# Five edits to the attention stage of a hybrid retention and dilated-attention decoder step

## The chip, the core and the metric

The kernel runs on one core of one Trainium2 chip. The metric is the device time of one execution in microseconds (us), the median of the runs. The engines go by the names that the profile gives them: PE is TensorE (matmuls; PEld its weight loads), DVE is VectorE, ACT is ScalarE, POOL is GpSimd, and SP is SyncE, which issues most DMAs.

## What is computed

One step of a one-layer decoder, for a prompt of 512 tokens and a sample group of 8 sequences with 8 new tokens each, 576 tokens in all. An RMSNorm and one input projection (1024 to 3584 columns) feed two groups of heads. Eight heads do retention (chunks of 128, a state that is carried on). Eight heads of width 64 do softmax attention over a mixture of dilated windows, with a distance penalty:

```python
BRANCHES = ((128, 1), (512, 4), (2048, 16))
for window, dil in BRANCHES:
    dist = dil * jnp.arange(window // dil + 1, dtype=jnp.int32)
    local = q_pos[:, None] - dist[None, :] - k_start
    ...
    s = jnp.einsum('bqhd,bqnhd->bhqn', qf, kg) - slopes[:, None, None] * dist
```

The prompt attends to its own keys; the sample attends to 1024 cached keys and values of each sequence and to its new ones. Both groups are concatenated, projected back and added; a gated feed-forward layer with a causal convolution of width 3 follows (1024 to 2 x 2816 and back), and a last RMSNorm. Outputs are the tokens, the retention states, the key and value caches with the new rows at their end, and the convolution's state. All data is fp32.

## The kernel before

Activations stand with features on partitions and the 576 tokens along the free dimension. A dense product (L254) splits weights and activations into a high and a low part of type fp32r and adds three products, high x high, high x low and low x high; each weight block of 128 x 128 meets two halves of 288 tokens, so a step of one 128-row block is six matmuls. ACT makes the high part of a weight chunk (L219), DVE the low part (L229), SP loads it (L211).

Work is written out as streams (Python generators) that a small planner, `Merge`, interleaves when the program is built. Each `yield a, b` says how much TensorE time was just written and how long to wait for other engines; a third number, where there is one, is the progress that counts in place of the first. Streams with an amount of work left (`mg.add(in_proj(), 130.0e3)`, `attn_prompt` 32.7e3, `attn_sample` 59.6e3) are served so that their progress relative to what is left stays equal. A stream that yields `None` waits until something else has moved on. Every engine then executes its instructions strictly in the order that the planner wrote.

After the retention part, three such streams share TensorE from about 150 to 336 us of the span:

- `in_proj` goes on with the projection. For the third and fourth pair of heads its attention sections wait until all six attention units of the pair two before (four of the prompt, two of the sample) are written.
- `attn_prompt` runs `attn_unit(hp, i)` for each pair of heads and each block i of 128 queries, sixteen units, at most two at once. A unit with i > 0 splits its queries into a high part `qa` and a rest `ql`, multiplies them with split keys (L764 with 128 rows, L766 with 64 rows each for the two heads), takes the softmax (exponential on ACT L780, reciprocals on DVE L783, both heads' weights scaled on POOL L785), transposes the weights (L791) and multiplies with the values (L804). n = 128 (i + 1) is the number of keys.
- `attn_sample` runs eight units of four sequences. For each sequence it loads a key tile `kc` (three buffers) and a value tile `vc` (six buffers) of 384 KB from the cache, each with three DMAs issued by SP (L861, L863), and transposes the keys (L877, copies L878). Then the unit multiplies queries with keys (L887), takes the softmax, transposes the weights (L910, and L911 for the 64 columns of new keys) and multiplies with the values (L923: four matmuls side by side in column groups of 32; the last step has only the 64 rows of new values). Just before a unit, POOL copies the new keys of its four sequences into their key tiles (L977).

`natural` transposes a section of 576 tokens back to rows (L495: four full blocks and one of 64 columns); `store_window` writes the new cache rows, with one DMA for each of the 8 sequences of the sample (L507). PSUM has two tiles of type `d` and four of type `m`; `room` and `give` count the latter. From 336 us on the program is output projection and feed-forward, and nothing in it is edited.

Of the kernel before, what the change touches and what calls it, by code (L numbers as in the profile page):

```python
# [18 lines left out]
P = 128  # L19
D = 1024  # L20
NP = 512
# [125 lines left out]
def decoder_step(ctx, tc, a):  # L147
# [147 lines left out]
    def rows_of(j):  # L295
        return (P, slice(j * P, (j + 1) * P)) if j < 4 else (NS, slice(NP, T))
# [191 lines left out]

    def natural(src, dst):

        yield from room(2)
        p1, p2 = mtile(), mtile()
        for j in range(5):
            r, s = rows_of(j)
            pe.transpose((p1[:, s] if j < 4 else p2[:NS, :P]), src[:, s], ident)  # L495
        yield 550.0, 300.0
        act.copy(dst[:, 0:4], p1.rearrange("p (j c) -> p j c", j=4))
        dve.tensor_copy(dst[:NS, 4], p2[:NS, :P])
        give(2)

    def store_window(nat, which, hp):
        c = slice(hp * P, (hp + 1) * P)
        op_ = a[f"o_w{which}_p"].rearrange("a (j p) h d -> p (a j) (h d)", p=P)[:, :, c]
        sp.dma_start(op_, nat[:, 0:4])
        os_ = a[f"o_w{which}_s"]
        for b in range(B):
            sp.dma_start(os_[b, PAST:PAST + TS].rearrange("t h d -> t (h d)")[:, c], nat[b * TS:(b + 1) * TS, 4])  # L507

# [12 lines left out]
    def in_post(m, ps):  # L521
# [12 lines left out]
        elif sec < 4:  # L534
# [10 lines left out]
            if sec in (1, 2):  # L545
                n = rp.tile([P, 5, P], F32, name=f"n{sec}", tag=f"n{sec}", bufs=2)
                yield from natural(t, n)
                r["kv"[sec - 1]] = n
# [3 lines left out]
        else:  # L552
# [8 lines left out]
            else:  # L561
                dve.tensor_mul(t, y, rstd_b)
                yield 0.0, 1700.0
                n = atp.tile([P, 5, P], F32, name=f"n{sec}", tag=f"n{sec}", bufs=1 if sec == 5 else 2)
                yield from natural(t, n)
                if sec == 6:
# [166 lines left out]
    half, used = {}, {}  # L733
    pbs, O, flying = {}, {}, {"p": 0, "s": 0}

# [5 lines left out]
    def attn_unit(hp, i):  # L741
# [3 lines left out]
        if i:  # L745

            q_ = A[hp][4][:, i * P:(i + 1) * P]
            qa = [kvb[0].tile([P, P], F32R, name=f"qa{h2}", tag=f"qa{h2}", bufs=2) for h2 in range(2)]
            ql = kvb[0].tile([P, P], F32R, name="ql", tag="ql", bufs=2)
            for h2, q in halves():  # L750
                act.copy(qa[h2][q], q_[q])
                act.copy(qa[h2][other(h2)], q_[q])
            yield 0.0, 1000.0
            for h2, q in halves():
                dve.tensor_sub(ql[q], q_[q], f32(qa[h2][q]))
            yield 0.0, 500.0
# [5 lines left out]
        else:  # L762
            for h2 in range(2):
                pe.matmul(pss[h2][:, :n], qa[h2], kk[hp][h2][:, :n], start=True, stop=False)  # L764
            for h2, q in halves():
                pe.matmul(pss[h2][:, :n], ql[q], kk[hp][h2][q, :n], start=False, stop=True)  # L766
        for ps in pss:
# [14 lines left out]
        for ps, s, c in S:  # L782
            dve.reciprocal(c[:, 2:3], c[:, 1:2])  # L783
        for ps, s, c in S:
            pool.tensor_scalar(s[:, :n], s[:, :n], c[:, 2:3], 1.0, op0=OP.mult, op1=OP.mult)  # L785
        yield 0.0, 2.5 * n + 300.0
        yield from room(2)
# [27 lines left out]

    kk, scored = {}, {}

# [32 lines left out]
    def attn_sample():  # L850
# [3 lines left out]
        def load(u, x, which):  # L854
# [5 lines left out]
            cols = slice(hp * P, (hp + 1) * P)  # L860
            sp.dma_start(t[:, 2:6], c[512:].rearrange("(j p) h d -> p j (h d)", p=P)[:, :, cols])  # L861
            for j in range(2):
                sp.dma_start(t[:, j], c[256 * j:256 * (j + 1)].rearrange("(m u) h d -> m u (h d)", u=16)[:, 0:8, cols])  # L863
            return t
# [5 lines left out]
        def keys(u, x):  # L870
# [8 lines left out]
            del K[u, x]  # L879
            KT[u, x] = kt  # L880

        def unit(u):
# [26 lines left out]
            for j in range(6):  # L909
                pe.transpose(ps[:, j * P:(j + 1) * P], s[:, j * P:(j + 1) * P], ident)  # L910
            pe.transpose(ps[:NS, KEYS:KEYS + P], s[:, SK:], ident)  # L911
            yield 770.0, 200.0
            pt = kvb[0].tile([P, 7, P], F32, name="spt", tag="spt", bufs=1)
            dve.tensor_copy(pt[:, :3].rearrange("p j q -> p (j q)"), ps[:, :384])
            act.copy(pt[:, 3:6].rearrange("p j q -> p (j q)"), ps[:, 384:KEYS])
            act.copy(pt[:NS, 6], ps[:NS, KEYS:KEYS + P])  # L916
            yield 0.0, 2200.0
            yield from room(1)
            ps = mtile()
            for j in range(7):  # L920
                for x in range(4):
                    n, v = (P, V[u, x][:, j]) if j < 6 else (NS, A[hp]["v"][:NS, 4])
                    pe.matmul(ps[x * 32:(x + 1) * 32, :P], pt[:n, j, x * 32:(x + 1) * 32], v, start=j == 0, stop=j == 6,  # L923
                              tile_position=(0, x * 32))
                if j == 3:
                    yield 900.0, 0.0
# [35 lines left out]
        for u in range(8):  # L962
            hp, g = units[u]
            for x in range(4):
                yield from room(2)
                keys(u, x)
                give(2)
                yield 660.0, 1600.0
                ahead(4 * u + x + 4, "k")
# [5 lines left out]
            for x in range(4):  # L975
                b = 4 * g + x
                pool.tensor_copy(KT[u, x][:, KEYS:], A[hp][5][:, NP + b * TS:NP + (b + 1) * TS])  # L977
            flying["s"] += 1
            mg.add(unit(u), None, 600.0)
            yield 0.0, 1000.0, 4100.0  # L980

# [17 lines left out]
    kvx = mid.enter_context(ExitStack())  # L999
    kvb.append(kvx.enter_context(tc.tile_pool(name="kv", bufs=2, reuse_waits="tile")))  # L1000

    MIX = [4, 5, 6, 7, 0, 1, 2, 3]
# [321 lines left out]
```

## Time and profile before

| what | value |
|---|---|
| runs of the kernel before | 829.95, 831.85, 833.71 us; median 831.85 us |
| profiled execution | 832.6 us, its span 830.8 us |
| mean granted TensorE clock | 0.994 |
| PE, share of the span with a matmul in flight | 98% |
| DVE / ACT / POOL busy | 50% / 36% / 18% |
| DMA | 128.68 MB, mean 155 GB/s |

The profiled execution is 0.75 us above the median and 1.8 us longer than its span. Matmuls overlap, so that a busy PE is not a PE at its best: what one costs is read from the distance between starts. PE also stands still while its sequencer waits, and then the weight load (PEld) of the next matmul shows the wait.

### The profile page before, as it was taken

How to read it: one execution, taken by the hardware profiler on the slowest of the kernel's cores; microseconds unless marked ns; L12 is line 12 of the kernel's file. 1: busy time of each engine (PE TensorE's matmuls, PEld its weight loads, DVE VectorE, ACT ScalarE, POOL GpSimd, SP SyncE). 2: the span in 40 equal slices, each digit the busy share in tenths (PEclk: the TensorE clock that was granted, in tenths of full speed). 3: DMA queues.
4: the chain of work that ended last, by engine and by line, in shares of the span. 5: the costliest groups of instructions: out<-in, count | busy, mean ns of one | idle time of the engine just before them, and what ended most of it. 6: DMA issues, size and time to landing. Idle time of an engine off the chain costs nothing.

```text
span 830.8 us, 15970 instructions
## 1 busy us (share of the span) xinstructions
PE 813.8 (98%) x6559; PEld 772.2 (93%) x6559; DVE 412.5 (50%) x792; ACT 295.3 (36%) x511; POOL 148.0 (18%) x234
## 2 busy tenths in 40 slices
PE   7999999999999999999999999999999999999995
PEld 6999999887887888999999999999999999999995
DVE  4664555665546456754545455432235545453333
ACT  5422232554446367333223323311223323342222
POOL 1321202011111113023122212100012322210111
PEclk9999999999999999999999999999999999999998
DMA  9354653658787774455265554543334445543213
GB/s 269 102 173 125 203 175 97 185 158 236 217 219 197 219 212 121 110 177 179 78 201 178 178 174 125 168 140 89 93 102 153 152 152 178 171 156 96 71 52 115
DMA packets 180247, 128.68 MB, mean 155 GB/s; under 512 B 15424, under 2 KB 176848, under 8 KB 179661
## 3 DMA queue, kind: packets, MB, share of 16 engines
q1 hardware_dynamic: 179021, 93.75, 40.3%
q10 hardware_dynamic: 928, 33.63, 11.2%
q8 instruction: 52, 0.85, 0.4%
q0 software_dynamic: 224, 0.28, 0.1%
q14 instruction: 22, 0.18, 0.1%
HBM read 121.52 MB, written 39.66 MB: 194 GB/s over the span
## 4 chain that ended last, share of the span: by engine, by line
PE 96%; ACT 1%; DVE 1%; DMA 0%; POOL 0%; issue 0%; ACTq 0%; DVEq 0%; POOLq 0%
PE d L254 75%; PE m L877 2%; PE m L923 2%; PE d L451 2%; PE m L804 1%; PE d L887 1%; PE m L791 1%; PE m L495 1%; PE px L410 1%; PE m L1214 1%; PE px L254 1%; PE m L663 1%; PE m L764 1%; PE d L910 1%; PE m L766 1%; PE m L627 1%
## 5 line engine op out<-in xcount | busy, mean ns | idle before, releaser
L219 ACT ACTIVATE whi<-wraw 128x1024 fp32r<-128x1024 f32 (+2 forms) x114 | 110.6, 970 | 364.9 <-issue 182.6
L229 DVE TENSOR_TENSOR wlo<-wraw,whi 128x1024 fp32r<-128x1024 f32 (+2 forms) x114 | 126.7, 1112 | 120.4 <-ACT whi L219 117.0
L254 PE MATMUL d<-bhi,whi 128*128 128x288 f32 x768 | 173.3, 307 | 0.0
L254 PE MATMUL d<-bhi,wlo 128*128 128x288 f32 x768 | 164.3, 295 | 0.0
L254 PE MATMUL d<-blo,whi 128*128 128x288 f32 x768 | 163.9, 295 | 0.0
L254 PE MATMUL d<-hhi,whi 128*128 128x288 f32 x704 | 150.9, 296 | 0.0
L254 PE MATMUL d<-hhi,wlo 128*128 128x288 f32 x704 | 150.8, 296 | 0.0
L254 PE MATMUL d<-hlo,whi 128*128 128x288 f32 x704 | 150.7, 296 | 0.0
L254 PEld LDWEIGHTS d<-bhi,whi 128*128 128x128 f32 x768 | 121.5, 189 | 5.2 <-issue 3.6
L254 PEld LDWEIGHTS d<-bhi,wlo 128*128 128x128 f32 x768 | 123.3, 188 | 0.0
L254 PEld LDWEIGHTS d<-blo,whi 128*128 128x128 f32 x768 | 123.2, 188 | 0.0
L254 PEld LDWEIGHTS d<-hhi,whi 128*128 128x128 f32 x704 | 113.4, 189 | 0.1
L254 PEld LDWEIGHTS d<-hhi,wlo 128*128 128x128 f32 x704 | 113.4, 189 | 0.0
L254 PEld LDWEIGHTS d<-hlo,whi 128*128 128x128 f32 x704 | 113.4, 189 | 0.0
L1122 DVE TENSOR_TENSOR ue<-d,rstd_b 128x512 f32<-128x512 f32 x22 | 15.2, 691 | 74.6 <-PE d L254 74.6
L1141 POOL TENSOR_TENSOR g<-g,cv 128x512 f32<-128x512 f32 x20 | 25.7, 1287 | 142.1 <-DVE g L1138 136.7
L785 POOL TENSOR_SCALAR s<-s,sc 128x128 f32<-128x128 f32 (+3 forms) x32 | 18.2, 575 | 141.1 <-DVE sc L783 139.9
L1038 POOL TENSOR_TENSOR acc<-acc,sq 128x576 f32<-128x576 f32 x13 | 20.9, 1607 | 104.2 <-ACT sq L1037 104.2
L1127 POOL COPY cout<-ue 128x2 f32<-128x2 f32 x22 | 5.7, 258 | 137.8 <-DVE ue L1122 137.8
L878 DVE COPY kt<-m 128x384 f32<-128x384 f32 x32 | 17.8, 556 | 22.4 <-PE m L877 21.2
L878 ACT COPY kt<-m 128x384 f32<-128x384 f32 x32 | 15.3, 477 | 38.4 <-PE m L877 36.8
L877 PE MATMUL m<-ident,kc 128*128 128x128 f32 x192 | 27.2, 277 | 0.9 <-ACT spt L916 0.9
(264 smaller groups left out, 1030.7 us busy)
## 6 DMA issues: line engine op xcount, KB each, us to landing
wraw<-in_w_up_dram SPq DMA_DIRECT2D x44, 512.0 KB
wraw<-in_w_in_dram SPq DMA_DIRECT2D x26, 512.0 KB
kc<-in_cache_win_k_dram SPq DMA_DIRECT2D x32, 256.0 KB
vc<-in_cache_win_v_dram SPq DMA_DIRECT2D x32, 256.0 KB
wraw<-in_w_down_dram SPq DMA_DIRECT2D x16, 384.0 KB
wraw<-in_w_down_dram SPq DMA_DIRECT2D x16, 320.0 KB
kc<-in_cache_win_k_dram SPq DMA_DIRECT2D x64, 64.0 KB
vc<-in_cache_win_v_dram SPq DMA_DIRECT2D x64, 64.0 KB
```

The costliest lines, as they stand in the source:

```text
L219: act.activation(split[i][0][:, c], raw[i][:, c], AF.Copy)
L229: dve.tensor_sub(lo[:, c], raw[i][:, c], f32(hi[:, c]))
L254: pe.matmul(ps[:, C0 + s * H2:C0 + (s + 1) * H2], wt[:, rows[k] if rows else k - k0], x[k][:, s * H2:(s + 1) * H2], start=first and k == k ...
L410: pe.transpose(ps[:, s], xn[:r, j, k * P:(k + 1) * P], ident[:r, :r])
L451: pe.matmul(ps[i][:, C0 + s * H2:C0 + (s + 1) * H2], wt[:, k], x[k][:, s * H2:(s + 1) * H2], start=k == 0 and wt is hi and x is xhis, stop ...
L785: pool.tensor_scalar(s[:, :n], s[:, :n], c[:, 2:3], 1.0, op0=OP.mult, op1=OP.mult)
L877: pe.transpose(ps[:, j * P:(j + 1) * P], K[u, x][:, 3 * w + j], ident)
L878: (act.copy if w else dve.tensor_copy)(kt[:, w * 384:w * 384 + 384], ps[:, :384])
L923: pe.matmul(ps[x * 32:(x + 1) * 32, :P], pt[:n, j, x * 32:(x + 1) * 32], v, start=j == 0, stop=j == 6, tile_position=(0, x * 32))
L1038: pool.tensor_tensor(acc, acc, sq, op=OP.add)
L1122: dve.tensor_mul(u[:, 2:NP + 2], ya[:, :NP], rstd_b[:, :NP])
L1141: eng.tensor_tensor(g[:, :NP], g[:, :NP], c[:, :NP], op=OP.mult)
```

## The change

1. **Value loads.** The three DMAs of a value tile are issued by POOL; those of a key tile stay on SP.
2. **Stores.** The eight stores of a section's new sample rows become one. For this the new rows stand in partitions 64 to 127 of the fifth block, and POOL clears partitions 0 to 63 there for the values, four times.
3. **Pace.** A key step counts 1685 of progress and the unit's start nothing more; before it was 660 for a key step and 4100 for the start. The sum for a unit is 6740 both times. The new keys are copied right behind each key step where they are there already.
4. **Prompt's weights.** Of the two scalings of a prompt unit, POOL does one and DVE the other; the planner's wait behind them goes from 2.5 n + 300 to 1.25 n + 500 ns.
5. **Full shapes.** The rest of the queries stands in two fixed tiles whose other halves are zero, so that L766 has 128 rows; a unit's split waits until the previous unit's L766 is written (`flying["ql"]`). The fifth transposes in `natural` and the last one in the sample's softmax take 128 columns, and the last step of L923 takes 128 rows of values, the lower 64 of them zero. One ACT copy takes the place of two (L915, L916).

```diff
-        for j in range(5):
-            r, s = rows_of(j)
-            pe.transpose((p1[:, s] if j < 4 else p2[:NS, :P]), src[:, s], ident)
+        for j in range(4):
+            pe.transpose(p1[:, j * P:(j + 1) * P], src[:, j * P:(j + 1) * P], ident)
+        pe.transpose(p2[:, :P], src[:, T - P:], ident)
...
-        dve.tensor_copy(dst[:NS, 4], p2[:NS, :P])
+        dve.tensor_copy(dst[rows, 4], p2[UP, :P])
...
-        for b in range(B):
-            sp.dma_start(os_[b, PAST:PAST + TS].rearrange("t h d -> t (h d)")[:, c], nat[b * TS:(b + 1) * TS, 4])
+        sp.dma_start(os_[:, PAST:PAST + TS].rearrange("b t h d -> b t (h d)")[:, :, c], nat[NS:, 4])
...
+                if sec == 6:
+                    pool.memset(n[:NS, 4], 0.0)
+                yield from natural(t, n, UP)
...
-            ql = kvb[0].tile([P, P], F32R, name="ql", tag="ql", bufs=2)
+            while flying["ql"]:
+                yield None
+            flying["ql"] = 1
...
-                dve.tensor_sub(ql[q], q_[q], f32(qa[h2][q]))
+                dve.tensor_sub(qls[h2][q], q_[q], f32(qa[h2][q]))
...
-                pe.matmul(pss[h2][:, :n], ql[q], kk[hp][h2][q, :n], start=False, stop=True)
+                pe.matmul(pss[h2][:, :n], qls[h2], kk[hp][h2][:, :n], start=False, stop=True)
+            flying["ql"] = 0
...
-        for ps, s, c in S:
-            pool.tensor_scalar(s[:, :n], s[:, :n], c[:, 2:3], 1.0, op0=OP.mult, op1=OP.mult)
-        yield 0.0, 2.5 * n + 300.0
+        for eng, (ps, s, c) in zip((pool, dve), S):
+            eng.tensor_scalar(s[:, :n], s[:, :n], c[:, 2:3], 1.0, op0=OP.mult, op1=OP.mult)
+        yield 0.0, 1.25 * n + 500.0
...
-            sp.dma_start(t[:, 2:6], c[512:].rearrange("(j p) h d -> p j (h d)", p=P)[:, :, cols])
+            eng = sp if which == "k" else pool
+            eng.dma_start(t[:, 2:6], c[512:].rearrange("(j p) h d -> p j (h d)", p=P)[:, :, cols])
             for j in range(2):
-                sp.dma_start(t[:, j], c[256 * j:256 * (j + 1)].rearrange("(m u) h d -> m u (h d)", u=16)[:, 0:8, cols])
+                eng.dma_start(t[:, j], c[256 * j:256 * (j + 1)].rearrange("(m u) h d -> m u (h d)", u=16)[:, 0:8, cols])
...
+        def new_keys(u, x):
+            hp, g = units[u]
+            b = 4 * g + x
+            if (u, x) not in early:
+                early.add((u, x))
+                pool.tensor_copy(KT[u, x][:, KEYS:], A[hp][5][:, NP + b * TS:NP + (b + 1) * TS])
...
-            pe.transpose(ps[:NS, KEYS:KEYS + P], s[:, SK:], ident)
+            pe.transpose(ps[:, KEYS:KEYS + P], s[:, SW - P:], ident)
...
-                    n, v = (P, V[u, x][:, j]) if j < 6 else (NS, A[hp]["v"][:NS, 4])
-                    pe.matmul(ps[x * 32:(x + 1) * 32, :P], pt[:n, j, x * 32:(x + 1) * 32], v, start=j == 0, stop=j == 6,
+                    v = V[u, x][:, j] if j < 6 else A[hp]["v"][:, 4]
+                    pe.matmul(ps[x * 32:(x + 1) * 32, :P], pt[:, j, x * 32:(x + 1) * 32], v, start=j == 0, stop=j == 6,
...
-                yield 660.0, 1600.0
+                yield 660.0, 1600.0, 1685.0
...
-            yield 0.0, 1000.0, 4100.0
+            yield 0.0, 1000.0
```

## Rows read from the trace of the kernel before

**Rows 1.** The page's chain that ended last, its shares by engine.
```profile
PE 96%; ACT 1%; DVE 1%; DMA 0%; POOL 0%; issue 0%; ACTq 0%; DVEq 0%; POOLq 0%
```

**Rows 2.** PE timeline of a prompt unit, n = 256: start, busy us, line, shapes, count.
```profile
166.58 0.42 PE L254 MATMUL d<-bhi,wlo 128*128 128x288 f32 x2
166.84 0.28 PE L764 MATMUL m<-kdec,qa 128*128 128x256 f32 x1
166.96 0.28 PE L764 MATMUL m<-ka,qa 128*128 128x256 f32 x1
167.17 0.38 PE L766 MATMUL m<-kdec,ql 64*128 64x256 f32 x1
...
167.48 0.54 PE L254 MATMUL d<-bhi,whi 128*128 128x288 f32 x2
167.85 0.30 PE L254 MATMUL d<-blo,whi 128*128 128x288 f32 x1
```

**Rows 3.** PE timeline of a prompt unit, n = 512.
```profile
269.27 0.39 PE L764 MATMUL m<-kdec,qa 128*128 128x512 f32 x1
269.51 0.39 PE L764 MATMUL m<-ka,qa 128*128 128x512 f32 x1
269.82 0.50 PE L766 MATMUL m<-kdec,ql 64*128 64x512 f32 x1
...
270.26 0.33 PE L938 MATMUL m<-ident,ob 128*128 128x128 f32 x1
```

**Rows 4.** PE timeline of a sample unit's product with the values.
```profile
244.31 1.52 PE L923 MATMUL m<-vc,spt 128*32 128x128 f32 x48
245.76 0.42 PE L923 MATMUL m<-n,spt 64*32 64x128 f32 x8
246.12 0.44 PE L495 MATMUL m<-ident,t 128*128 128x128 f32 x2
```

**Rows 5.** PE groups by form: line, shapes, count, busy us, mean ns, idle before.
```profile
L910 PE MATMUL d<-ident,ss 128*128 128x128 f32 x48 | 6.6, 274 | 0.0
...
L911 PE MATMUL d<-ident,ss 128*64 128x128 f32 x8 | 2.2, 273 | 0.0
```

**Rows 6.** Waits of PEld, 150 to 336 us: total us, times, longest.
```profile
PEld m L791 <- POOL s L785: 1.8, 7, 0.4
PEld d L887 <- POOL kt L977: 1.8, 3, 1.2
```

**Rows 7.** POOL groups by form.
```profile
L977 POOL COPY kt<-t 128x8 f32<-128x8 f32 x32 | 5.6, 220 | 0.2
...
L785 POOL TENSOR_SCALAR s<-s,sc 128x512 f32<-128x512 f32 x8 | 5.5, 692 | 30.4 <-DVE sc L783 30.4
```

**Rows 8.** DVE groups by form, the sample's own scaling.
```profile
L902 DVE TENSOR_SCALAR ss<-ss,ssc 128x776 f32<-128x776 f32 x8 | 5.2, 651 | 0.3
```

**Rows 9.** POOL timeline: four key copies; two scalings of 384 columns.
```profile
232.40 1.64 POOL L977 COPY kt<-t 128x8 f32<-128x8 f32 x4
...
264.81 2.11 POOL L785 TENSOR_SCALAR s<-s,sc 128x384 f32<-128x384 f32 x2 [4.80 <-DVE sc L783]
```

**Rows 10.** POOL timeline at the start: DMAs of 4 and of 128 rows.
```profile
3.56 0.50 POOL L353 DMA_DIRECT2D vrows<-in_ret_gn_b_dram  x1
4.05 0.58 POOL L355 DMA_DIRECT2D small<-in_c_small_dram  x1
```

**Rows 11.** SP timeline: the eight stores of one section's sample rows.
```profile
163.78 4.17 SPq L507 DMA_DIRECT2D out_dram<-n  x8
```

**Rows 12.** PE timeline of the stretch without dense work.
```profile
193.96 0.82 PE L877 MATMUL m<-ident,kc 128*128 128x128 f32 x6
...
196.97 0.92 PE L877 MATMUL m<-ident,kc 128*128 128x128 f32 x6 [0.88 <-ACT spt L916]
...
203.99 0.51 PE L254 MATMUL d<-bhi,whi 128*128 128x288 f32 x2
```

**Rows 13.** Windows: us, PE, PEld, DVE, ACT, POOL busy (x instructions), clock, DMA.
```profile
194.00:204.00 10.00, 8.33 (x94) 6.53 (x92) 5.38 (x14) 4.52 (x13) 1.25 (x6) 0.83 0.86 245
```

More of the change, by code (lines that the diff above doesn't have):

```diff
@@ L487, in decoder_step, with natural @@
     rp = rpx.enter_context(tc.tile_pool(name="ret", bufs=2, reuse_waits="tile"))
-    def natural(src, dst):
+    UP = slice(NS, P)
+    def natural(src, dst, rows):
         yield from room(2)
         p1, p2 = mtile(), mtile()
-        for j in range(5):
-            r, s = rows_of(j)
-            pe.transpose((p1[:, s] if j < 4 else p2[:NS, :P]), src[:, s], ident)
+        for j in range(4):
+            pe.transpose(p1[:, j * P:(j + 1) * P], src[:, j * P:(j + 1) * P], ident)
+        pe.transpose(p2[:, :P], src[:, T - P:], ident)
         yield 550.0, 300.0
         act.copy(dst[:, 0:4], p1.rearrange("p (j c) -> p j c", j=4))
-        dve.tensor_copy(dst[:NS, 4], p2[:NS, :P])
+        dve.tensor_copy(dst[rows, 4], p2[UP, :P])
         give(2)
@@ L546, in in_post @@
                 n = rp.tile([P, 5, P], F32, name=f"n{sec}", tag=f"n{sec}", bufs=2)
-                yield from natural(t, n)
+                yield from natural(t, n, slice(0, NS))
                 r["kv"[sec - 1]] = n
@@ L564, in in_post @@
                 n = atp.tile([P, 5, P], F32, name=f"n{sec}", tag=f"n{sec}", bufs=1 if sec == 5 else 2)
-                yield from natural(t, n)
+                if sec == 6:
+                    pool.memset(n[:NS, 4], 0.0)
+                yield from natural(t, n, UP)
                 if sec == 6:
@@ L733, in decoder_step @@
     half, used = {}, {}
-    pbs, O, flying = {}, {}, {"p": 0, "s": 0}
+    pbs, O, flying = {}, {}, {"p": 0, "s": 0, "ql": 0}
     def load_bias(hp):
@@ L814, in attn_unit @@
         flying["p"] -= 1
-    kk, scored = {}, {}
+    kk, scored, qls = {}, {}, []
     def k_split(hp):
@@ L880, in keys @@
             KT[u, x] = kt
+            if hp in A and 5 in A[hp]:
+                new_keys(u, x)
+        early = set()
+        def new_keys(u, x):
[4 more added lines that the diff above has]
+                pool.tensor_copy(KT[u, x][:, KEYS:], A[hp][5][:, NP + b * TS:NP + (b + 1) * TS])
         def unit(u):
@@ L914, in unit @@
             dve.tensor_copy(pt[:, :3].rearrange("p j q -> p (j q)"), ps[:, :384])
-            act.copy(pt[:, 3:6].rearrange("p j q -> p (j q)"), ps[:, 384:KEYS])
-            act.copy(pt[:NS, 6], ps[:NS, KEYS:KEYS + P])
+            act.copy(pt[:, 3:7].rearrange("p j q -> p (j q)"), ps[:, 384:KEYS + P])
             yield 0.0, 2200.0
@@ L975, in attn_sample @@
             for x in range(4):
-                b = 4 * g + x
-                pool.tensor_copy(KT[u, x][:, KEYS:], A[hp][5][:, NP + b * TS:NP + (b + 1) * TS])
+                new_keys(u, x)
             flying["s"] += 1
             mg.add(unit(u), None, 600.0)
-            yield 0.0, 1000.0, 4100.0
+            yield 0.0, 1000.0
     last_in = []
@@ L1000, in decoder_step @@
     kvb.append(kvx.enter_context(tc.tile_pool(name="kv", bufs=2, reuse_waits="tile")))
+    for h2 in range(2):
+        qls.append(kvb[0].tile([P, P], F32R, name=f"ql{h2}", bufs=1))
+        pool.memset(f32(qls[h2][other(h2)]), 0.0)
     MIX = [4, 5, 6, 7, 0, 1, 2, 3]
```

## The prediction

> **What bounds the kernel now.** I read first the chain of work that ended last: PE holds 96% of it and no DMA has a share [rows 1]. So the question for every edit is whether PE executes less, or waits less. Busy time can't tell that here, since matmuls overlap; I read distances between starts on PE's timeline. From 336 us on nothing is edited, so the whole effect lies in the 186 us from 150 to 336, where projection, prompt attention and sample attention are interleaved. There I looked for three things: what a shape costs beside a full one [rows 2 to 5], what PE waits for [rows 6], and where the dense work that covers all waits is missing [rows 12, 13]. PE's list of waits in this stretch has no DMA.
>
> **Full shapes, the rest of the queries.** In a unit with n = 256 the two full matmuls start 0.12 and 0.21 us before the next one, the pair with 64 rows takes 0.31 to the next work, and the first two dense matmuls behind it take 0.37 where a steady pair takes 0.26 [rows 2]. So each change between 128 and 64 rows costs about 0.1, and the pair costs more than two full matmuls. Four full ones would take 4 x 0.12 = 0.48 for 0.64: 0.16 saved, and 0.11 more where dense work follows. With n = 512 it is 0.24 + 0.31 + 0.44 = 0.99 against 4 x 0.24 = 0.96: 0.03 saved [rows 3]; n = 384 I put halfway, 0.10. Four pairs of heads make 4 x 0.29 = 1.2 us without the dense part and 1.2 + 12 x 0.11 = 2.5 with it everywhere. I take two cases in three: **-2.1 us**.
>
> The pair's second matmul starts with its first, yet the two take 0.31 us where a full one takes 0.12 [rows 2]. The Trainium skill speaks against this edit (TensorE: Matmul & The Clock Gate, Part 3: Packing small matmuls): matmuls in different row groups run at once, so a pair would cost what one matmul does. By that rule the pair is 0.12, 0.18 and 0.24 us, the full shape adds as much, 4 x 0.54 = 2.2 us, and the sum below would end at 829.2 + 2.1 + 2.2 = 833.5; the row shows the concurrent start but not the price, so I give this way no chance.
>
> **Full shapes, the values.** 48 matmuls of L923 take 1.45 us, the last 8 with 64 rows 0.36 [rows 4]. At the pace of the first, 8 take 1.45 x 8 / 48 = 0.24. Eight units save 8 x 0.12 = **-1.0 us** (bound: nothing, if the 0.36 is all the step to what follows). The transposes of 64 columns cost what full ones do, 273 against 274 ns [rows 5]: nothing.
>
> **Prompt's weights.** PE waits 1.8 us in 7 places for POOL's scalings [rows 6]. With 512 keys POOL takes 0.69 for each head, 1.39 for both [rows 7]; DVE's 776 columns take 0.65 [rows 8], so 512 some 0.43 (estimate, by columns). Side by side both are ready after 0.69, and all 1.8 could go. But the planner also writes the transposes 1580 - 1140 = 440 ns earlier, and POOL and DVE don't always run side by side: four key copies of 0.22 each [rows 7] took 1.64, two scalings of 384 columns 2.11 where 512 take 1.39 [rows 7, 9]. One after the other they take 0.69 + 0.43 = 1.12, 0.27 earlier than now, and PE would come 0.17 too early, at worst 16 x 0.17 = 2.7 us. Between -1.8 and +2.7 I take **-0.7**. DVE's own time for it, 16 x 0.43 = 7 us, is spread over 186 us of an engine that is half idle: nothing; without that cover it would be late with low parts of weights, which are made a chunk ahead.
>
> **New keys.** L887 waits 1.8 us for POOL's key copies, in three places [rows 6], since they stand in a burst before the unit, behind scalings. Copied at each key step, three of four are out of the way. The fourth can still stand behind a value load. Bounds 0 and -1.8, I take half: **-0.9**.
>
> **Value loads on POOL.** 96 DMAs leave SP and 96 come to POOL, which waits in its order for a free value buffer; behind it stand the scalings, the key copies and the copies of the sample's queries, and PE waits for all three. The trace has POOL DMAs of 4 rows at 0.50 and of 128 rows at 0.58 us [rows 10]. The two small loads have 128 rows of 512 bytes: 0.58 each. The large one has 512 such pieces: at least 0.58, by the slope of the two rows 0.83, at most four times 0.58 = 2.3. A tile then holds POOL for 1.75 to 3.5 us; the rows lie near the slope, so I take 2.0. 32 tiles make 64 us in 186. A scaling meets one with a chance of 0.34 and waits 1.0 on average: 16 x 0.34 = 5.5 us if all of it reached PE. It does not: the scaling comes at the end of a chain DVE, ACT, DVE and POOL is idle before it, so most loads that stand ahead of it are done by then. I take **+2.0**; bounds are 0 and, with 3.5 us a tile (share 0.6, mean rest 1.75), 16 x 0.6 x 1.75 = 17 us.
>
> **What costs nothing.** SP: a store takes 4.17 / 8 = 0.52 us of its issue [rows 11]; 56 stores and 96 value loads fewer are 79 us by that price, but PE waits for no DMA, and weights have three buffers. The loads' bytes stay; DMA engines are 0.86 busy in the worst stretch [rows 13], and a value tile is asked for long before its product. Were it late, L923 would stand. The four clears and the joint ACT copy are small and off the path. The wait for `ql` holds a unit's split until the previous L766 is written; behind it on DVE stand PSUM copies, but at most two units fly, and the earlier L766 is long written.
>
> **Pace.** A unit's start came after 2640 of progress in key steps, now after 6740; 4100 of the stream's 53.9 thousand, 7.6% of 186 us, is up to 14 us later. The projection waits for sample units, and that shows: from 193.96 to 203.99 there is no dense matmul [rows 12], PE stands 0.88 us once, and the clock averages 0.83, where 1.7 of 10 us are lost [rows 13]. That is 2.6 us in 10. A later unit makes it longer; evenly spread key copies on ACT and DVE make the pauses in it fewer. I take 0; bounds -2.6 and 2 places x 14 x 0.26 = +7.4.
>
> **The sum.** -2.1 - 1.0 - 0.7 - 0.9 + 2.0 = -2.7 us. The profiled execution is 832.6, 1.8 over its span and 0.75 over the median; the difference goes to the median: 831.85 - 2.7 = **829.2 us**.
>
> **The rivals.**
> *All waits covered.* Value loads cost PE nothing, and POOL's waits go: -2.5 - 1.0 - 1.8 - 1.8 = -7.1, 824.7; with the dense-free stretch mended too, 822. For it: POOL is only 18% busy. Against: 64 us are new on it.
> *POOL becomes what PE waits for (slower).* If the load of 512 pieces takes near 2.3 us and two thirds of the 17 us reach PE, +11 - 4.7: 838. It turns the sign when these waits pass 4.7 us and shows at 8.9. For it: POOL and DVE block each other already [rows 9]. The Trainium skill (SBUF — State Buffer, Who interferes with whom) says that POOL can't write DMA descriptors while DVE holds their shared ports; no POOL DMA of the trace runs beside such work.
> *The pace starves the projection.* Half of the bound, +3.7: 832.9. It cancels the gain at 10 us more without dense work.
> *The two engines take turns.* The scalings give 0 to +1 instead of -0.7: 829.9 to 831. The same section of the Trainium skill makes this a rule for a DVE scaling within SBUF beside any POOL instruction; by it the scalings stand in turn in all 16 units.
>
> **Chances.** Forecast 34% (827 to 831.3), all covered 32%, POOL 16%, pace 12%, turns 6%. A measurement of this kernel tells about 0.5%, 4.2 us: faster is under 827.7, slower over 836.0. Faster: 10 of the forecast and 31 of the covered, 41%. Slower: 13 of POOL and 3 of pace, 16%. Same: 43%. The range from 822, the covered end, to 838 leaves out less than 2 in 10: a mended stretch beyond that, or POOL's bound of 17.
>
> **What would show it.** Right: L766 as full matmuls 0.12 to 0.24 apart; 56 matmuls of L923 in about 1.7 us; POOL DMAs of 0.6 and 0.8 us; fewer waits of L791. Wrong: large POOL DMAs over 1.4 us; L791 or L887 waiting behind a value load; stretches without L254 longer than 10 us, or a second fall of the clock. The stage's end, 336 us now, carries the sum: near 333.

## The result: slower by 0.85%, and the profile after

The changed kernel takes 839.08 us (median of 6 runs, 836.99 to 840.33) where the kernel before takes 831.56 beside it: ratio 1.0085, 95% interval 1.0063 to 1.0107 (taken over all runs; that of the two medians is 1.0090). The forecast was 829.2, and 838 its upper end. Below, 0.001 of a ratio is 0.83 us, and runs from different chips are compared by their ratio to the kernel before.

The stage that was to end near 333 us ends at 342.4 instead of 335.6 (start of the last L955, before L938). The page's chain of waits shows who holds the end. Where PE had 96% and DMA 0 [rows 1], it reads now:

```profile
PE 92%; ACT 2%; DMA 2%; issue 1%; DVE 1%; POOL 0%; SPq 0%; ACTq 0%; DVEq 0%; POOLq 0%
```

Line numbers moved with the edits. In the changed kernel the prompt's scores are L766 for a first block (L761 before) and L769 and L771 for the others (L764, L766), its scalings L791 (L785), its transposes L797 (L791); loads are L868 and L870 (L861, L863), key transposes L884 (L877), new keys L898 (L977), queries with keys L905 (L887), the sample's weight transposes L928 and L929 (L910, L911), its product with the values L940 (L923) and its last transpose L955 (L938).

The shapes did what was said of them. PE's timeline of the changed kernel, a unit with n = 256 and one product with the values:

```profile
212.08 0.28 PE L771 MATMUL m<-kdec,ql 128*128 128x256 f32 x1
212.20 0.28 PE L771 MATMUL m<-ka,ql 128*128 128x256 f32 x1
212.32 0.42 PE L254 MATMUL d<-bhi,whi 128*128 128x288 f32 x2
212.58 0.42 PE L254 MATMUL d<-blo,whi 128*128 128x288 f32 x2
...
252.79 1.52 PE L940 MATMUL m<-vc,spt 128*32 128x128 f32 x48
254.12 0.40 PE L940 MATMUL m<-n,spt 128*32 128x128 f32 x8
254.45 0.77 PE L884 MATMUL m<-ident,kc 128*128 128x128 f32 x5
```

The pair L771 takes 0.24 us to the next work (0.31 before, [rows 2]), the dense pair behind it 0.26 (0.37), and the 56 matmuls of L940 take 1.66 (1.81, [rows 4]). Of these 0.15 us, 0.12 lie in the 48 matmuls before the change of shape (1.33 for 1.45); the last eight take 0.33 for 0.36. What PE waits for is the other half of the story. Waits of PE, 150 to 345 us: total us, times, longest.

```profile
PE m L797 <- POOL s L791: 2.4, 1, 2.4
PE m L884 <- DVE sc L779: 1.8, 2, 1.1
PE m L884 <- DMA kc<-in_cache_win_k_dram: 1.6, 1, 1.6
PE d L254 <- ACT spt L933: 1.5, 1, 1.5
PE d L254 <- DVE ssc L912: 1.3, 1, 1.3
```

Only the first is of a kind that the prediction priced, and there it was 0.4 us at most at one time [rows 6]; the others are new. Two, those for the key tile and for POOL's scaling, are followed by a fall of the granted clock. The windows of the changed kernel (us, busy us of PE, PEld, DVE, ACT and POOL, clock, DMA share, GB/s) hold the first fall, 3.4 us from 161.8, and the second, 3.4 us from 206.2; the kernel before had one [rows 13].

```profile
160.00:170.00 10.00, 8.77 (x62) 7.41 (x63) 4.96 (x16) 4.27 (x13) 2.44 (x5) 0.83 1.12 276
198.00:210.00 12.00, 8.43 (x97) 6.25 (x95) 6.97 (x20) 6.06 (x18) 5.09 (x11) 0.86 0.89 209
```

So the stage can be split. "Waits" are the distances between starts on PE above 0.4 us from 150 us to the stage's end, each less 0.2; "clock" is half of the time at 1.2 GHz; the rest is what is left of the stage's end, in us. They are those of one execution each: single executions show a mean granted clock of 0.992 to 0.996 in the changed kernel and 0.992 to 0.998 in the kernel before, so a fall in one needn't be in the next.

| kernel | stage's end | waits | clock | rest |
|---|---|---|---|---|
| before | 335.6 | 8.0 | 1.7 | 325.9 |
| after | 342.4 | 15.8 | 3.4 | 323.2 |

The rest is 2.7 us shorter, near the 3.1 forecast for the shapes. It is a rough number: before_stores below executes the same matmuls in the same order as the kernel before, and its rest is 327.4, 1.5 us more. What was gained was lost to 7.8 us of new waits and 1.7 of clock.

### The profile page after: what moved, and what is told of

Same layout as the page of the kernel before. It is cut to its first block, busy times and chain, and to the rows that moved or that the text cites. A ratio compares the mean times of both kernels' runs of the same rounds, so it can differ in the third digit from the quotient of the medians.

```text
span 838.5 us, 15896 instructions
## 1 busy us (share of the span) xinstructions
PE 812.7 (97%) x6559; PEld 775.0 (92%) x6559; DVE 418.9 (50%) x808; ACT 294.9 (35%) x503; POOL 201.5 (24%) x320
## 4 chain that ended last, share of the span: by engine, by line
PE 92%; ACT 2%; DMA 2%; issue 1%; DVE 1%; POOL 0%; SPq 0%; ACTq 0%; DVEq 0%; POOLq 0%
PE d L254 73%; PE m L884 2%; PE d L451 2%; PE m L940 2%; PE d L905 1%; PE m L810 1%; PE m L797 1%; DMA kc<-in_cache_win_k_dram 1%; PE px L410 1%; PE m L1233 1%; PE m L496 1%; PE px L254 1%; PE m L666 1%; PE m L769 1%; PE m L630 1%
## 5 line engine op out<-in xcount | busy, mean ns | idle before, releaser
L254 PE MATMUL d<-bhi,whi 128*128 128x288 f32 x768 | 172.7, 306 | 2.8 <-ACT spt L933 1.5
L254 PE MATMUL d<-bhi,wlo 128*128 128x288 f32 x768 | 164.8, 296 | 0.0
L254 PE MATMUL d<-blo,whi 128*128 128x288 f32 x768 | 164.4, 296 | 0.0
L254 PE MATMUL d<-hhi,whi 128*128 128x288 f32 x704 | 150.9, 296 | 0.0
L254 PE MATMUL d<-hhi,wlo 128*128 128x288 f32 x704 | 150.8, 296 | 0.0
L254 PE MATMUL d<-hlo,whi 128*128 128x288 f32 x704 | 150.7, 296 | 0.0
L254 PEld LDWEIGHTS d<-bhi,whi 128*128 128x128 f32 x768 | 122.6, 190 | 6.7 <-issue 3.4
L254 PEld LDWEIGHTS d<-bhi,wlo 128*128 128x128 f32 x768 | 123.9, 189 | 0.0
L254 PEld LDWEIGHTS d<-blo,whi 128*128 128x128 f32 x768 | 123.8, 189 | 0.0
L254 PEld LDWEIGHTS d<-hhi,whi 128*128 128x128 f32 x704 | 113.4, 189 | 0.1
L254 PEld LDWEIGHTS d<-hhi,wlo 128*128 128x128 f32 x704 | 113.4, 189 | 0.0
L254 PEld LDWEIGHTS d<-hlo,whi 128*128 128x128 f32 x704 | 113.4, 189 | 0.0
L870 POOL DMA_DIRECT2D vc<-in_cache_win_v_dram x64 | 35.0, 554 | 4.0 <-DMA vc<-in_cache_win_v_dram 4.0
L884 PE MATMUL m<-ident,kc 128*128 128x128 f32 x192 | 28.3, 282 | 3.4 <-DVE sc L779 1.8
L868 POOL DMA_DIRECT2D vc<-in_cache_win_v_dram x32 | 26.1, 817 | 21.7 <-PE m L940 20.6
```

The lines of the kernel that those rows point to most:

```text
L254: pe.matmul(ps[:, C0 + s * H2:C0 + (s + 1) * H2], wt[:, rows[k] if rows else k - k0], x[k][:, s * H2:(s + 1) * H2], start=first and k == k ...
L868: eng.dma_start(t[:, 2:6], c[512:].rearrange("(j p) h d -> p j (h d)", p=P)[:, :, cols])
L870: eng.dma_start(t[:, j], c[256 * j:256 * (j + 1)].rearrange("(m u) h d -> m u (h d)", u=16)[:, 0:8, cols])
L884: pe.transpose(ps[:, j * P:(j + 1) * P], K[u, x][:, 3 * w + j], ident)
```

## The experiments

Each run is one or a few edits away from the kernel before or after. In the table, ratio is to the kernel before, with its 95% interval; the other columns are those above, of the profiled execution. By the traces, TensorE's matmuls stand in the same order in before, b_full, b_pool, before_stores and three_nowait; in b_full_wait, a_three, three_st8, three_vpool and three_two; in after and a_vsp; and in a_scal and a_yield. Between two runs of one such group only the other engines' work differs, or the shapes.

| run | what it is | ratio | end | waits | clock |
|---|---|---|---|---|---|
| b_full | before + full shapes | 0.9997 (0.9980 to 1.0013) | 336.1 | 9.8 | 1.7 |
| b_full_wait | the same + wait for `ql` | 1.0033 (1.0021 to 1.0045) | 338.4 | 12.8 | 0 |
| b_pool | before + value loads on POOL | 1.0079 (1.0063 to 1.0095) | 342.9 | 13.1 | 1.7 |
| before_stores | before + single stores | 0.9980 (0.9966 to 0.9994) | 334.8 | 7.4 | 0 |
| a_three | after, three edits undone | 0.9949 (0.9935 to 0.9963) | 332.2 | 7.6 | 0 |
| three_nowait | a_three without wait for `ql` | 0.9936 (0.9919 to 0.9953) | 333.2 | 6.9 | 0 |
| three_st8 | a_three with eight stores | 1.0047 (1.0031 to 1.0062) | 342.5 | 17.3 | 1.7 |
| three_vpool | a_three with value loads on POOL | 0.9959 (0.9945 to 0.9974) | 333.9 | 9.3 | 0 |
| three_pace | a_three with the even pace | 0.9986 (0.9974 to 0.9999) | 333.9 | 9.9 | 0 |
| three_yield | a_three with the shorter planned wait | 0.9989 (0.9975 to 1.0003) | 334.4 | 10.5 | 0 |
| three_two | a_three with two engines | 0.9971 (0.9957 to 0.9985) | 334.2 | 9.2 | 1.7 |
| a_vsp | after, value loads on SP | 1.0044 (1.0027 to 1.0062) | 339.8 | 14.1 | 3.4 |
| a_pace | after, old pace | 1.0024 (1.0013 to 1.0036) | 336.7 | 12.4 | 0 |
| a_scal | after, scalings as before | 1.0010 (0.9999 to 1.0021) | 337.1 | 10.5 | 0 |
| a_yield | after, old planned wait | 1.0024 (1.0011 to 1.0037) | 338.1 | 12.6 | 0 |
| after_mid | after, planned wait in between | 1.0051 (1.0033 to 1.0070) | 339.9 | 13.7 | 3.4 |
| wait_early | after, shorter wait in pairs 1 and 2 only | 1.0048 (1.0032 to 1.0063) | 341.3 | 16.0 | 1.7 |
| wait_late | after, shorter wait in pairs 3 and 4 only | 1.0022 (1.0009 to 1.0035) | 336.3 | 12.6 | 0 |

**Value loads.** Two runs, one from each side:

```diff
 a_vsp (from after)
-            eng = sp if which == "k" else pool
+            eng = sp
 b_pool (from before), both DMA lines
-            sp.dma_start(t[:, 2:6], c[512:].rearrange("(j p) h d -> p j (h d)", p=P)[:, :, cols])
+            eng = sp if which == "k" else pool
+            eng.dma_start(t[:, 2:6], c[512:].rearrange("(j p) h d -> p j (h d)", p=P)[:, :, cols])
```

> The changed kernel with the value loads back on SP; TensorE's order is that of the changed kernel, instruction for instruction. Theory 1, the value loads on GpSimd cost the time (their packets compete with the key loads: PE waits 1.6 us for a key tile at 159 us, then the clock falls at 161.8; GpSimd is held): the first wait and the first fall go, the stage ends at 337 to 338 instead of 342.4, 833 to 835 us. Theory 2, the new order of the streams costs it (pace, shorter wait behind the scalings, ql): no change, 838 to 840. If SP is short of issue time, slower than 840.

> The kernel before with the value loads on GpSimd and nothing else; TensorE's order is that of the kernel before. Theory 1: 4 to 6 us slower than before, 836 to 838, with PE waiting for a key tile near 159 us and a second fall of the clock. Theory 2: within 2 us of before, 830 to 834. The prediction's term was +2.0.

On POOL the loads cost 6.6 us in the order before and 3.4 in the order after (1.0085 against 1.0044), so theory 1 holds for a part; about half of the loss, 3.7 of 7.1 us, stays with the loads on SP, as theory 2 says. In b_pool neither sign of theory 1 shows: PE waits for no key tile, and the clock falls once, as in the kernel before. What holds PE there is in its waits and on POOL's timeline (lines L888 and L978 there are L905 and L898 of after):

```profile
PE d L888 <- POOL kt L978: 5.1, 4, 2.0
```

```profile
189.86 0.79 POOL L862 DMA_DIRECT2D vc<-in_cache_win_v_dram  x1
190.64 1.07 POOL L864 DMA_DIRECT2D vc<-in_cache_win_v_dram  x2
191.75 0.57 POOL L978 COPY kt<-t 128x8 f32<-128x8 f32 x4
```

```profile
188.96 1.07 PE L888 MATMUL d<-kt,qb 128*32 128x512 f32 x8
191.99 0.94 PE L888 MATMUL d<-kt,qb 128*32 128x264 f32 x7 [1.96 <-POOL kt L978]
```

The planner writes a value tile's load with the last key step, and the unit's key copies straight behind it. It is no chance meeting: PE stands there in four of the eight units, 1 to 2 us each. (Its weight loads show the same stops as 11.4 us; the 16 us in an expectation below add the two.) The changed kernel has the copies ahead of the loads, and its list has no wait of L905 for POOL. What is left of the price shows at one place. From 150.3 to 157.6 us POOL asks for three value tiles beside SP's key loads; the last of the three DMAs of a key tile lands late, PE stands 1.55 us at 161.23, and the clock falls. In a_vsp, where SP asks for the same tiles from 153.0 to 162.8, neither shows; its clock falls later, from 201.4 to 208.2. three_vpool below has the same stop, 1.30 us at 161.24, without the fall. Whether it is the tiles' bytes or their earlier start that delays the key tile was not tested. PE's timeline of after:

```profile
159.35 0.33 PE L884 MATMUL m<-ident,kc 128*128 128x128 f32 x1
161.23 0.85 PE L884 MATMUL m<-ident,kc 128*128 128x128 f32 x5 [1.55 <-DMA kc<-in_cache_win_k_dram]
```

**Pace and scalings undone in the changed kernel.**

```diff
 a_pace
-                yield 660.0, 1600.0, 1685.0
+                yield 660.0, 1600.0
-            yield 0.0, 1000.0
+            yield 0.0, 1000.0, 4100.0
 a_scal (a_yield: the second pair of lines only; after_mid: 1.9 * n + 400.0)
-        for eng, (ps, s, c) in zip((pool, dve), S):
-            eng.tensor_scalar(s[:, :n], s[:, :n], c[:, 2:3], 1.0, op0=OP.mult, op1=OP.mult)
+        for ps, s, c in S:
+            pool.tensor_scalar(s[:, :n], s[:, :n], c[:, 2:3], 1.0, op0=OP.mult, op1=OP.mult)
-        yield 0.0, 1.25 * n + 500.0
+        yield 0.0, 2.5 * n + 300.0
```

> The changed kernel with the old pace of a unit (660 for a key step, 4100 at its start). Theory 2: the stretch without dense work at 198 to 210 us shrinks from 12.3 to about 10 us, the wait of 2.4 us for POOL's scaling in it and the fall of the clock at 206 become those of the kernel before, 834 to 836 us. Theory 1: only the order moves, the waits behind the value loads stay, 837 to 840.

> The changed kernel with both scalings on GpSimd and the old planned wait of 2.5 n + 300 behind them. If the planned wait became too short (transposes written before their weights are there; PE waits 2.4 us once for the scaling at 204 us, and for ACT and DVE at 174, 218, 224 and 241): 1 to 3 us faster, 836 to 838. If the two engines were worth what was predicted: 0.7 slower, 839 to 840. Theory 1: the scalings stand behind value loads on GpSimd twice as long, 840 to 842.

> The changed kernel with only the planned wait behind the scalings put back to 2.5 n + 300; DVE still does one of the two. If the planned wait alone makes the 6 us between the changed kernel and the run with the old scalings: 833 to 835. If DVE's share does it (DVE's copies of keys come late behind it): 838 to 840. If it is the order at large, any value between.

> The changed kernel with a planned wait between the two, 1.9 n + 400. If transposes come too early, the cost follows the wait: halfway between 1.0024 and 1.0085 of before, 1.004 to 1.007. If the cost is the order at one place (the stretch without dense work and what follows), it jumps: near one of the two ends or beyond them.

The old pace gives back 5.1 us, about what was expected, the old scalings 6.2, more than that, and 5.1 of the 6.2 come from one number of the planner, the wait. The profiles of a_pace, a_scal and a_yield have no fall of the clock. Halfway between the two waits lies 1.0051, between the two results, but its interval reaches both, so the time decides for neither expectation; its profile has the long stretch without dense work of after (12.6 us from 195.1; a_yield: 9.4 from 196.3).

**Shapes alone, and the wait for `ql`.** b_full takes the shape edits and the joint ACT copy into the kernel before, with eight stores and without the wait; b_full_wait has the wait too (the three added lines before the matmul):

```diff
-            ql = kvb[0].tile([P, P], F32R, name="ql", tag="ql", bufs=2)
+            while flying["ql"]:
+                yield None
+            flying["ql"] = 1
-                pe.matmul(pss[h2][:, :n], ql[q], kk[hp][h2][q, :n], start=False, stop=True)
+                pe.matmul(pss[h2][:, :n], qls[h2], kk[hp][h2][:, :n], start=False, stop=True)
```

> The kernel before with the full shapes only (rest of the queries, values, fifth transposes, joint copy) and without the wait for ql. As priced in the prediction: 2.1 + 1.0 faster, 829 to 830 us where before is 832.7; the stage ends near 332.5 us instead of 335.6. If the pairs of 64 rows ran at once and cost what one matmul costs: 1 to 2 us slower, 834 to 835.

> The run with the full shapes only, with the wait for ql as in the change. If the wait is free, as predicted: equal to that run. If it costs (a unit's split and scores come one slot later, the order of TensorE moves): 1 to 4 us slower than that run.

Both expectations of b_full failed: no gain and no loss. Its rest is 1.3 us shorter than before's, but PE's list has a wait that the kernel before had not (in b_full_wait it is 4.1 us):

```profile
PE m L884 <- DMA kc<-in_cache_win_k_dram: 2.7, 2, 2.0
```

The order of the matmuls is that of the kernel before, so a faster PE asks for key tiles sooner than SP delivers them. The wait for `ql` costs 3.0 us more here; it does move the order.

**Three edits undone, and one put back at a time.** a_three is after with value loads on SP, old pace and old scalings: full shapes with the wait for `ql`, early key copies and single stores stay. The lines of the others are those shown above, and for the stores:

```diff
 three_st8 (from a_three)
-        sp.dma_start(os_[:, PAST:PAST + TS].rearrange("b t h d -> b t (h d)")[:, :, c], nat[NS:, 4])
+        for b in range(B):
+            sp.dma_start(os_[b, PAST:PAST + TS].rearrange("t h d -> t (h d)")[:, c], nat[NS + b * TS:NS + (b + 1) * TS, 4])
```

> The changed kernel without three edits: value loads on SP, old pace, both scalings on GpSimd with the old planned wait. What stays: full shapes with the wait for ql, early new keys, single stores. If those three edits hold the whole loss: the prediction's terms -2.1 - 1.0 - 0.9, 828.5 to 829.5 us. If the rest has a cost of its own (the wait for ql): 831 to 834.

> The run without three edits (828.2 us), without the wait for ql. If the wait costs what it cost with the full shapes alone (835.3 against 833.0): 826 to 827. If it only moved the order, and the key loads were the cost there: 828 to 829.

> The run without three edits (828.2 us), with eight stores for a section again. If SP's time is what made key tiles late in the runs with the full shapes alone (PE waits 2.7 and 4.1 us for them): 832 to 835, with these waits back. If the early key copies made the 7 us between those runs: 828 to 829. The prediction gave the single stores nothing.

> The kernel before with single stores and nothing else. The prediction's price: nothing, 0.998 to 1.001. If SP's issue time already holds the key tiles back in the kernel before, where no wait for them shows: faster, 0.993 to 0.997.

> The run without three edits (828.2 us), with the value loads on GpSimd again; TensorE's order is that of 828.2. Theory 1a, the value loads cost because key copies stand right behind them on GpSimd (16 us of waits of L888 in the run with the value loads alone): those copies are early here, so 828 to 829. Theory 1b, they cost because their bytes come in a burst beside the key loads: PE waits for a key tile once near 159 us, 830 to 833.

> The run without three edits (828.2 us), with the even pace. If the pace costs by itself (units start later, stretches without dense work get longer): 831 to 834. If the pace hurts only together with the shorter wait behind the scalings: 828 to 830. The prediction's bounds for it were -2.6 and +7.4.

> The run without three edits (828.2 us, 0.995 of before) with the shorter planned wait of 1.25 n + 500 behind the scalings, which both stay on GpSimd. If the shorter wait costs by itself, transposes written before their weights are there: 5 us more as between the runs of the even pace, 1.000 to 1.002 of before, with more waits of L797 for the scaling. If it costs only with the even pace, through the long stretch without dense work: 0.994 to 0.997.

> The run without three edits with the scalings on two engines, the old planned wait kept: the edit as it was priced, without its wait. As predicted by the rows, PE's waits of 1.8 us for the scalings go: 0.993 to 0.995 of before. If the engines take turns or DVE comes late for the key copies: 0.996 to 0.998.

a_three came out as the prediction's terms say, 828.2 us, but by luck: the shapes alone gave nothing, and the single stores, priced at nothing, are in it. three_nowait, 5.3 us under before, has the lowest ratio here; a_three lies within its interval. The surprise is three_st8: eight stores instead of one cost 8.2 us. Early copies and single stores are all that lies between b_full_wait and a_three, and three_st8, which has the early copies, is as slow as b_full_wait; so the stores are it, with TensorE's order the same in all three. SP's queue in three_st8 shows how (L869, L871 are the loads; L509 the eight stores), with PE's answer:

```profile
215.20 0.54 SPq L506 DMA_DIRECT2D out_dram<-n  x1
215.83 2.74 SPq L509 DMA_DIRECT2D out_dram<-n  x8
...
219.12 0.53 SPq L869 DMA_DIRECT2D kc<-in_cache_win_k_dram  x1
219.69 1.19 SPq L871 DMA_DIRECT2D kc<-in_cache_win_k_dram  x2
...
222.86 0.54 SPq L869 DMA_DIRECT2D kc<-in_cache_win_k_dram  x1
```

```profile
224.28 0.30 PE L885 MATMUL m<-ident,kc 128*128 128x128 f32 x1 [2.14 <-DMA kc<-in_cache_win_k_dram]
225.86 0.88 PE L885 MATMUL m<-ident,kc 128*128 128x128 f32 x5 [1.27 <-DMA kc<-in_cache_win_k_dram]
```

From 209.75 to 226 us each issue starts within 0.1 us of the end of the one before: SP is a full queue, and a key load stands behind 3.3 us of stores (L506 and L508 take 1.2 in a_three). Over 150 to 310 us SP's issues fill 84% of the time in three_st8, 79% in a_three, and 85% in the kernel before. PE waits 7.5 us for key tiles in five places and 1.5 for a value tile, in a_three never, and behind the wait at 225.86 the clock falls for 3.4 us. In the kernel before the same relief is worth 1.7 us (before_stores), at the edge of what the expectation called nothing; no key tile was late there, and what its profile lacks is the fall of the clock.

With this in order, value loads on POOL cost 0.8 us (three_vpool, the intervals overlap). The even pace costs 3.1, the shorter wait alone 3.3, two engines alone 1.8 (overlapping intervals). In three_two PE's weight loads wait 0.7 us for POOL's scalings instead of a_three's 1.6, as forecast, but PE waits 1.7 us each for DVE's `t` (L557) and `sc` (L779), where it was 1.2 and 0.9: what POOL gives up, DVE's other work pays. PE's busy time in the same stretch of a_three and of three_pace:

```profile
190.00:212.00 22.00, 22.00 (x230) 1.00 0.80 221
```

```profile
190.00:212.00 22.00, 19.70 (x203) 1.00 0.72 201
```

In a_three, dense work goes on between the sample's pieces there; in three_pace there is none for 9.5 us from 193.5, and PE has new waits, of L928 for DVE (1.1 us) and of L254 for ACT's `spt` (0.9).

**Where the shorter wait loses it.** The edit of wait_early; wait_late has `hp > 1` in place of `hp < 2`:

```diff
-        yield 0.0, 1.25 * n + 500.0
+        yield 0.0, 1.25 * n + 500.0 if hp < 2 else 2.5 * n + 300.0
```

> The changed kernel with the shorter planned wait only in the units of the first two pairs of heads (to about 245 us) and 2.5 n + 300 in the others. If the cost lies in the long stretch without dense work at 198 to 210 us, with PE's wait of 2.4 us and the fall of the clock there: as the changed kernel, 1.007 to 1.009 of before. If it is spread over all units: 1.005 to 1.006.

> The changed kernel with the shorter planned wait only in the units of the last two pairs of heads. If the cost lies in that stretch: as the run with 2.5 n + 300 everywhere, 1.002 to 1.003 of before. If it is spread over all units: 1.005 to 1.006.

wait_late equals a_yield: the shorter wait costs nothing in the last two pairs. wait_early costs 2.2 us over it (their intervals just overlap) and has the stretch of 12.4 us and the wait of 2.4, as after has. It is below after (1.0048 against 1.0085; the intervals meet at 1.0063), although its matmuls stand as in after up to 290 us; after_mid, which has the stretch too, is at 1.0051. So neither expectation fits whole: some 2 of the 5.1 us go with the stretch, and the other 3 are not placed. PE's timeline of this stretch, first a_yield, then after:

```profile
201.10 0.72 PE L766 MATMUL m<-t,t 64*128 64x128 f32 x4 [0.39 <-DVE kt L885]
201.75 1.52 PE L940 MATMUL m<-vc,spt 128*32 128x128 f32 x48
203.09 0.40 PE L940 MATMUL m<-n,spt 128*32 128x128 f32 x8
203.42 1.23 PE L884 MATMUL m<-ident,kc 128*128 128x128 f32 x6
205.30 0.63 PE L797 MATMUL m<-ident,s 128*128 128x128 f32 x2 [0.65 <-POOL s L791]
205.68 0.51 PE L254 MATMUL d<-bhi,whi 128*128 128x288 f32 x2
```

```profile
201.70 0.49 PE L766 MATMUL m<-t,t 64*128 64x128 f32 x4
202.68 1.08 PE L940 MATMUL m<-vc,spt 128*32 128x128 f32 x32 [0.48 <-PE m L766]
206.19 0.71 PE L797 MATMUL m<-ident,s 128*128 128x128 f32 x2 [2.43 <-POOL s L791]
206.83 1.08 PE L940 MATMUL m<-vc,spt 128*32 128x128 f32 x16
207.68 0.65 PE L940 MATMUL m<-n,spt 128*32 128x128 f32 x8
208.27 1.49 PE L884 MATMUL m<-ident,kc 128*128 128x128 f32 x6
```

From L766 to L797 it takes 4.2 us in a_yield and 4.5 in after, the time of scores, softmax and scaling. In a_yield PE does the product with the values and a key step meanwhile. In after the planner put the two transposes inside that product, so that 24 of its 56 matmuls and the key step wait behind them; then the clock is at half rate until 209.6. This unit has n = 128, for which the planned wait became longer (660 for 620): it is the order that moved, through the units before.

## Why the prediction was wrong, step by step

The chain a_three's relatives make adds up to the result: shapes, early copies and single stores -5.3 us (three_nowait), the wait for `ql` +1.1 (a_three), the even pace +3.1 (three_pace), scalings with their shorter wait +4.8 (a_vsp), value loads on POOL +3.4 (after), in sum +7.1. It closes by construction, and a step's size depends on what is in place before it: taken out of the changed kernel singly, the scalings are worth 6.2, the pace 5.1 and the value loads 3.4.

Forecast -2.7 and measured +7.1 lie 9.8 us apart. By this chain 5.5 of them are the prompt's weights, 3.1 the pace, 1.4 the value loads and 1.1 the wait for `ql`; shapes, new keys and stores came out 1.3 better than their -4.0. So the steps that failed are the prompt's weights and the pace. The first was priced as waits at single units, and the runs show that its shorter wait moves the order of the planner; of the second the mechanism was seen and its price set to nothing. Of the prediction's signs of being wrong, two came, the dense-free stretch of 12.3 us and a second fall of the clock; the POOL DMAs of over 1.4 us did not.

- **Full shapes, -3.1.** The sizes held on PE's timeline (1.81 - 1.66 = 0.15 us for a product with the values, 0.12 forecast), though for the values by another way: the eight matmuls take 0.33 us and not 0.24, and the gain lies in the step to them. As time they were worth nothing alone (0.9997), since the key tiles came too late. The rule of the Trainium skill that was weighed here (TensorE: Matmul & The Clock Gate, Part 3: Packing small matmuls) had the full shape dearer by 2.2 us; the row above disagrees, with 0.24 us for the pair where it was 0.31.
- **"SP: ... by that price, but PE waits for no DMA".** This step failed too, but the other way: it hid a gain, and doesn't explain the loss. That PE waited for no DMA was true of the kernel before, and the step took it for slack. But SP had little: its issues fill 85% of the stretch, and a key tile's DMAs stand in one line with all stores and loads. Single stores, priced at nothing, are worth 1.7 us by themselves and 8.2 in a_three's order; with the early copies they are 5.1 beside full shapes in the order before (three_nowait against b_full).
- **Prompt's weights, -0.7.** Failed: +4.8 with its wait. The bound of +2.7 took 0.17 us at each of 16 units; the runs show one place where PE stands 2.4 us, and what comes after it. Of the parts, the wait costs 3.3 to 5.1 us, the second engine 1.2 to 1.8, which the intervals hardly tell from nothing. "Side by side both are ready after 0.69" didn't hold either. In the four units with 512 keys it takes 0.97 to 1.12 us, near the 1.12 of one after the other. In two of the four the second head's reciprocal waits for its exponential on ACT; in 9 of the 16 units DVE starts in the last 0.06 us of POOL's scaling. POOL and DVE in the changed kernel:

```profile
236.90 0.69 POOL L791 TENSOR_SCALAR s<-s,sc 128x512 f32<-128x512 f32 x1 [2.13 <-DVE sc L789]
237.34 0.16 DVE L789 RECIPROCAL sc<-sc 128x1 f32<-128x1 f32 x1 [0.54 <-ACT s L786]
237.54 0.48 DVE L791 TENSOR_SCALAR s<-s,sc 128x512 f32<-128x512 f32 x1
```

Where two scalings of 512 columns overlap almost whole, the later one is longer: DVE's takes 0.89 us at 189.47, POOL's 0.97 at 334.68. That is the rival of turns in part, in two of the four units.

- **Pace, "I take 0".** Failed: +3.1 in a_three's order, +5.1 in after's, inside the bound of +7.4, and by the way that the rival named it, stretches without dense work. The mechanism stood in the prediction, with the price of a microsecond of it; the failed part is the choice of 0 between the bounds, which let a hoped-for gain from evener pauses balance it.
- **Value loads, +2.0.** The issue price was right, 0.82 + 2 x 0.55 = 1.92 us a tile for 2.0. What it costs depends on what stands behind: 6.6 us with the key copies behind it, 3.4 in the changed kernel, 0.8 in a_three's order. The prediction let scalings meet loads by chance, and did not see that key copies meet them by the order written. This is the slower rival by its sign, not by its place, and its 838 lies near the measured 839 by chance: it needed large loads of 2.3 us, and they took 0.82. The Trainium skill's rule on ports (SBUF — State Buffer, Who interferes with whom), cited there, doesn't show in the issues: the 32 large loads took 0.79 to 0.85 us each beside a DVE that was half busy, and the two that ran 0.47 us beside a DVE scaling of 512 columns took 0.85.
- **New keys, -0.9.** Not seen as a gain by themselves (three_st8 has them, b_full_wait not, 1.0047 and 1.0033, in the same order of matmuls). What they do is take the copies from behind the value loads.
- **The wait for `ql`, 0.** +3.0 us in the order before, +1.1 in a_three's (within the intervals). It moved units by a slot and so the order.

What stays open: why the shorter wait moved the order just so, and where the 3 us between wait_early and after lie.

## What to carry to other kernels

Before you price an issue queue's relief at nothing, look whether its issues stand end to end: a queue without gaps is a second bound close under the first, and an edit that speeds the first engine up is paid out only when the queue is relieved with it. In an order that a planner writes, a constant that looks like a delay of 0.4 us moves other work by several; price it by the place with the least cover, where one early instruction holds back what would have hidden its wait, not by a mean over all units. A second engine halves a pair of operations only if both inputs are ready together. Test such bundles edit by edit in both directions: here the good edits were worth 5 us, and the three that cost 11 hid them.

## What the runs showed of the hardware

The value tiles go in far fewer and larger packets when POOL asks for them. By queue (packets, MB, share of 16 engines), in a_vsp and in after, which differ in nothing else:

```profile
q1 hardware_dynamic: 178573, 93.75, 40.0%
...
q0 software_dynamic: 224, 0.28, 0.1%
```

```profile
q1 hardware_dynamic: 152461, 81.16, 35.2%
...
q0 software_dynamic: 4832, 12.86, 5.5%
```

That is 12.6 MB in 26,112 packets on SP's queue, about 480 bytes each, against some 4,600 of 2.7 KB, for the same pieces of 512 bytes. And while three such tiles were in flight, SP's own issues of a key tile were slow: two DMAs that take 1.18 us for the same tile in a_vsp took 3.7 in after, and three_vpool shows the same. Single key loads of over 1 us stand in the other runs too, up to 1.9 in the kernel before, so the cause is not shown. First after, then a_vsp:

```profile
157.62 1.66 SPq L868 DMA_DIRECT2D kc<-in_cache_win_k_dram  x1
159.32 3.72 SPq L870 DMA_DIRECT2D kc<-in_cache_win_k_dram  x2
```

```profile
159.23 0.53 SPq L868 DMA_DIRECT2D kc<-in_cache_win_k_dram  x1
159.80 1.18 SPq L870 DMA_DIRECT2D kc<-in_cache_win_k_dram  x2
```
